# A hybrid decoder trunk on one core: the output projection's products move to another PSUM ring, the top-k search takes its bits out by shift and xor, and attention advances by more steps per feed-forward unit

## The chip, the cores and the metric

The kernel runs as one program on one NeuronCore of a Trainium2 chip. The metric is the time of one execution on the device, in microseconds (us). The core has five engines that run side by side, each through its own list of instructions in order: TensorE (PE in the profile; PEld are its weight loads) multiplies matrices into PSUM, VectorE (DVE), ScalarE (ACT) and GpSimd (POOL) do the elementwise work, and SyncE (SP) starts most DMA transfers. An engine waits where an input, or a buffer to write to, isn't ready.

## The reference

A sequence of 1024 tokens of width 1024 goes through two layers. Each has a token mixer and a squared-ReLU feed-forward part ("MLP" below), with RMS norms before and after. Layer 0 mixes with a state-space model (S5), layer 1 with sparse attention. Everything is float32.

```python
for i in range(2):
    pre = rms_norm(h, g[i, 0])
    mix = s5_mixer(pre, ...) if i == 0 else dsa_mixer(pre, w_in, w_out)
    h = h + rms_norm(mix, g[i, 1])
    ff = square(relu(rms_norm(h, g[i, 2]) @ w1[i])) @ w2[i]        # 1024 -> 4096 -> 1024
    h = h + rms_norm(ff, g[i, 3])

def dsa_mixer(h, w_in, w_out):                                      # 16 heads, 4 key heads, 8 index heads
    q, k, v, qi, ki, wi = split(h @ w_in); rope on q, k, qi, ki
    for each block of 128 queries:
        score = sum over index heads of relu(qi . ki) * wi          # causal
        idx = top 256 keys of each query by score
        o = softmax(q . k[idx] / 8) @ v[idx]
    return o @ w_out                                                # the output projection
```

## The kernel before

**Tiling.** The sequence is cut into two halves of 512 tokens. Activations lie with features on the 128 partitions, so a product of a 128x128 weight piece and 512 tokens is one matmul. A float32 product is made of three passes (`mm3`, lines 157 to 159): weights and activations are split into a high and a low part, and high x high, high x low and low x high add up in PSUM. `unit` loads 128x1024 weights and splits them: ScalarE makes the high part (line 140), VectorE or GpSimd the low part (line 141). One unit feeds 24 matmuls.

**Stages.** S5 for both halves; the MLP of layer 0 for half 0; the MLP of layer 0 for half 1, beside which the index projection, the projections and the attention of half 0 run; the MLP of layer 1 for half 0, beside which those of half 1 run; and the MLP of layer 1 for half 1 alone. Blocks 0 to 3 of 128 queries belong to half 0, blocks 4 to 7 to half 1.

**What runs beside an MLP.** `mlp` takes a generator (`side`). After each of its 64 units it advances the generator by `per` steps, and the instructions of these steps are given a priority ahead of the MLP's. `PER_B` lists the steps per unit for the stages beside layer 1's first MLP: projections with scores, search over blocks 4 and 5, scores of 6 and 7, search over 6 and 7 with attention of 4 and 5, attention of 6 and 7. `hold(n)` makes the generator wait for n units. What order the instructions of an engine finally have is set by a scheduler of the framework, which goes by priorities, by dependences, and by the pools: each tag of a pool has some buffers, given out in turn.

**PSUM.** The MLP's products take tiles of the tag `m` (`pm`, 3 buffers, "m" in the profile). Scores, attention, projections and the rope transposes of `att_r` take tiles of the tag `p1` (`p1`, "p" in the profile). Norms take tiles of the tag `c`.

**The norms between the MLPs.** When the MLP of layer 0 ends for half 1, `post_norm` sums squares (VectorE line 191, then small matmuls on line 194), takes the reciprocal root (lines 165 to 169), spreads it with transposes (line 236), copies it (ScalarE, line 238), scales (line 250) and adds the residual (line 260). `pre_norm` then scales by the gain (lines 206 and 207) and sums squares again (lines 184 to 194, line 212). `att_r` multiplies the rope tables by the norm's factor (line 1144) and transposes them (line 1153). Behind it in the program stand `att_out`, the output projection of half 0's attention, whose 8 tiles come from 24 matmuls each and leave PSUM by ScalarE (line 1124), and `index` for half 1. The same `att_out` runs a second time, for half 1, at the end of the generator.

**The search.** `topk` finds the 256th largest score of each query by bits. The score's bit pattern, as an integer, is built from bit 30 down. For each bit, `cand` is the current value with that bit set (line 966); VectorE counts the scores at or above it in one block (line 936), ScalarE in the other by summing signs of score minus candidate (line 974, for which line 970 makes the negative candidate); line 979 compares the two counts with what is wanted, and line 980 copies the candidate over the current value where the count suffices. There are three searches of two blocks each, 31 bits each.

## Time and profile before

| | |
|---|---|
| time, median of 3 runs | 2286.31 us (2282.1 to 2287.16) |
| the profiled execution: time, span | 2287.54 us, 2285.6 us |
| granted clock of TensorE, mean over the span | 0.971 |
| TensorE busy | 2166.6 us (95%), 10376 matmuls |
| VectorE busy | 1436.7 us (63%) |
| ScalarE busy | 1083.0 us (47%) |
| GpSimd busy | 701.8 us (31%) |

Lines of a timeline read: start in us, duration in us, engine, line, operation, written tile <- read tiles, size of an operand, count; in square brackets the idle time of the engine before it, and what ended that. Rows of a table by shape read: line, engine, operation, tiles, shapes, count, then busy us in all and mean ns of one, then idle us ahead of them and its main cause. A window's row reads: from:to, length, then for each engine the busy us and the number of instructions, and at the end the granted clock, the DMA engines' share and GB/s. A busy TensorE is also one that runs at half its clock, so a window is to be read with the clock beside it.

### The profile page before, as it was taken

Reading aid. Unit: us, or ns where it says so; the run is one execution under the profiler, and the core shown is the slowest. Engines: PE = TensorE matmul, PEld = TensorE weight load, DVE = VectorE, ACT = ScalarE, POOL = GpSimd, SP = SyncE. Lnnn points to the kernel's source line nnn. Section 1 sums busy time; section 2 is a strip of 40 time slices with the busy share of each in tenths; the row PEclk is TensorE's granted clock in tenths of the full one; section 3 lists DMA queues with packets and bytes.
Section 4 is the critical chain, followed back from the end, with each engine's and each line's share of the span. In section 5 each row is a group of like instructions: output and inputs, shape, how many; then the busy total and the mean of one; then the engine's idle time right before and its main releaser. Section 6 shows DMA issues by size and latency. Waiting matters only on the chain.

```text
span 2285.6 us, 29529 instructions
## 1 busy us (share of the span) xinstructions
PE 2166.6 (95%) x10376; PEld 1785.5 (78%) x10376; DVE 1436.7 (63%) x2775; ACT 1083.0 (47%) x2027; POOL 701.8 (31%) x588
## 2 busy tenths in 40 slices
PE   6999999999989999999988988999999899999996
PEld 3577778888878888888877766888788687888886
DVE  9566953333656598555677898989767467332335
ACT  4434643333353475555363455677457354423332
POOL 2004542222336522221346533221210035222223
PEclk9999999999999999999989999999999999999998
DMA  7002533333337653445346543433332444433231
GB/s 276 27 30 83 181 123 94 100 95 100 111 114 204 165 134 107 119 101 167 132 159 157 154 119 81 110 86 92 88 84 60 134 131 164 138 95 99 93 105 51
DMA packets 115893, 266.81 MB, mean 117 GB/s; under 512 B 14241, under 2 KB 49569, under 8 KB 115745
## 3 DMA queue, kind: packets, MB, share of 16 engines
q1 hardware_dynamic: 101984, 240.80, 33.9%
q0 software_dynamic: 12672, 23.07, 5.3%
q8 instruction: 82, 1.34, 0.3%
q10 hardware_dynamic: 1088, 1.05, 0.1%
q14 instruction: 67, 0.54, 0.1%
HBM read 229.02 MB, written 34.67 MB: 115 GB/s over the span
## 4 chain that ended last, share of the span: by engine, by line
PE 73%; DVE 15%; ACT 6%; issue 4%; DMA 1%; POOL 1%; SPq 0%; ACTq 0%; DVEq 0%; POOLq 0%
PE m L158 18%; PE m L157 18%; PE m L159 18%; PE p L1036 2%; PE p L1056 2%; PE p L157 2%; PE p L159 2%; PE p L158 2%; DVE wh L141 2%; PE p L1064 1%; DVE b L250 1%; PE p L1065 1%; ACT junk L974 1%; DVE b L207 1%; PE m L611 1%
## 5 line engine op out<-in xcount | busy, mean ns | idle before, releaser
L157 PE MATMUL m<-b,wh 128*128 128x512 f32 (+1 forms) x2208 | 860.5, 392 | 26.1 <-DVE acc L334 9.7
L158 PE MATMUL m<-b,wh 128*128 128x512 f32 (+1 forms) x2208 | 858.0, 391 | 4.6 <-DVE b L207 4.0
L159 PE MATMUL m<-b,wh 128*128 128x512 f32 (+1 forms) x2208 | 856.3, 390 | 4.3 <-DVE wh L141 4.3
L141 POOL TENSOR_TENSOR wh<-wr,wh 128x512 fp32r<-128x512 f32 (+1 forms) x346 | 448.7, 1302 | 1281.6 <-ACT wh L140 1261.6
L140 ACT ACTIVATE wh<-wr 128x512 fp32r<-128x512 f32 (+1 forms) x692 | 400.0, 592 | 503.2 <-PE m L159 413.9
L157 PEld LDWEIGHTS m<-b,wh 128*128 128x128 f32 x2208 | 419.4, 190 | 115.8 <-DVE acc L334 10.8
L159 PEld LDWEIGHTS m<-b,wh 128*128 128x128 f32 x2208 | 418.9, 190 | 88.8 <-DVE wh L141 5.1
L158 PEld LDWEIGHTS m<-b,wh 128*128 128x128 f32 x2208 | 419.2, 190 | 87.3 <-DVE b L207 4.8
L141 DVE TENSOR_TENSOR wh<-wr,wh 128x512 fp32r<-128x512 f32 (+1 forms) x346 | 273.4, 797 | 296.8 <-ACT wh L140 283.2
L334 DVE TENSOR_TENSOR acc<-acc,m 128x512 f32<-128x512 f32 x216 | 147.1, 682 | 155.5 <-PE m L159 153.5
L299 ACT ACTIVATE b<-m 128x512 f32<-128x512 f32 x128 | 76.2, 595 | 179.0 <-PE m L159 175.8
L148 DVE CAST b<-b 128x1024 fp32r<-128x1024 f32 x68 | 59.9, 881 | 135.5 <-ACT b L301 126.4
L159 PE MATMUL p<-b,wh 128*128 128x512 f32 (+1 forms) x304 | 116.1, 391 | 8.4 <-DVE wh L141 8.4
L157 PE MATMUL p<-b,wh 128*128 128x512 f32 (+1 forms) x304 | 115.8, 398 | 5.7 <-ACT b L721 3.4
L158 PE MATMUL p<-b,wh 128*128 128x512 f32 (+1 forms) x304 | 117.3, 391 | 0.0
L1043 ACT ACTIVATE s<-s,ring 128x128 f32<-128x128 f32 (+7 forms) x128 | 98.6, 772 | 36.6 <-DVE ring L1040 35.4
L1061 DVE TENSOR_TENSOR pt<-p,pt 128x512 fp32r<-128x512 f32 (+1 forms) x160 | 99.1, 630 | 22.3 <-ACT pt L1060 22.0
L1060 ACT ACTIVATE pt<-p 128x512 fp32r<-128x512 f32 (+1 forms) x160 | 83.5, 551 | 60.4 <-PE p L1056 59.5
L974 ACT ACTIVATE junk<-b,ring 128x512 bf16<-128x512 f32 (+2 forms) x90 | 80.7, 896 | 64.8 <-DVE ring L970 59.4
L1036 PE MATMUL p<-kt,q 128*128 128x512 f32 (+2 forms) x384 | 100.2, 365 | 1.5 <-DVE pt L1061 1.2
L1056 PE MATMUL p<-con,s 128*128 128x128 f32 x576 | 93.1, 273 | 0.0
L1040 DVE CUSTOM_DVE_ANT_0 s<-p,nb 128x512 f32<-128x512 f32 (+3 forms) x128 | 72.6, 582 | 25.4 <-PE p L1036 25.2
(304 smaller groups left out, 2738.0 us busy)
## 6 DMA issues: line engine op xcount, KB each, us to landing
wr<-in_w_dram SPq DMA_DIRECT2D x256, 512.0 KB, 3.6
wr<-in_wa_dram SPq DMA_DIRECT2D x32, 512.0 KB, 3.7
q<-qd POOLq DMA_DIRECT2D x64, 256.0 KB, 5.4
ld<-hd SPq DMA_DIRECT2D x24, 512.0 KB, 6.2
hd<-b SPq DMA_DIRECT2D x16, 512.0 KB, 4.4
qd<-b SPq DMA_DIRECT2D x128, 64.0 KB, 2.1
wr<-in_wao_dram SPq DMA_DIRECT2D x16, 512.0 KB, 3.6
q<-qi POOLq DMA_DIRECT2D x24, 256.0 KB, 4.8
```

The lines of the kernel that those rows point to most:

```text
L140: nc.scalar.activation(ph, pr, AF.Copy)
L141: (nc.gpsimd if h else nc.vector).tensor_sub(pl, pr, ph.bitcast(F32))
L157: mm(ps, w[0], x[0], start=start, stop=False)
L158: mm(ps, w[0], x[1], start=False, stop=False)
L159: return mm(ps, w[1], x[0], start=False, stop=stop)
L334: nc.vector.tensor_add(acc[d][:, j], acc[d][:, j], ps)
L974: nc.scalar.activation(junk[:, 1, :W[j]], keys[j].bitcast(F32), AF.Sign, bias=neg[:, j:j + 1], accum_out=cnt[:, j:j + 1])
L1036: nc.tensor.matmul(ps[:, :m], qt[:, v, 2 * hp + k, :], self.K[c][g // 2][:, g % 2, :m], start=v == 0, stop=v == 1)
L1043: nc.scalar.activation(s, s, AF.Exp, bias=least, scale=-1.0, accum_out=self.sums[:, h:h + 1])
L1056: nc.tensor.transpose(pt[:, kk, k, :], P[k][:, (k0 + kk) * 128:(k0 + kk + 1) * 128], self.ident)
L1060: nc.scalar.activation(ph[:, :nk], pt[:, :nk], AF.Copy)
L1061: nc.vector.tensor_sub(pl[:, :nk], pt[:, :nk], ph.bitcast(F32)[:, :nk])
```

## The change

It has three parts. In `topk`, the current value starts at 1<<30 and is itself the candidate. For each bit an xor prepares the value with the next lower bit set; the counts are now of scores below the candidate, and where too many are below, one instruction shifts the comparison's 1 to the bit's place and takes the bit out by xor. ScalarE gets its sign of candidate minus score by a scale of -1, so no negative candidate is made. `att_out` takes its PSUM tiles from `p1` and no longer from `m`, in both of its calls. And the steps per MLP unit become (8, 7, 8, 7, 6), with four units of hold ahead of half 1's `att_in`, 4 steps per unit from there, and one unit in each hold of `att_in`, as before.

```diff
-PER_B = (7, 6, 7, 6, 6)
+PER_B = (8, 7, 8, 7, 6)
-WAIT_OUT = 1
+WAIT_OUT = 4
...
-        def count(dst, j, thr):
-            ts(junk[:, 0, :W[j]], scs[j], thr, None, op0=ALU.is_ge, op1=ALU.add, accum_out=dst[:, j:j + 1])
+        def count(dst, j, thr, op=ALU.is_ge):
+            ts(junk[:, 0, :W[j]], scs[j], thr, None, op0=op, op1=ALU.add, accum_out=dst[:, j:j + 1])
...
-        kap2 = self.small([128, 4], F32, "kept")
+        lim, lim2 = [self.small([128, 4], F32, "kept") for _ in range(2)]
         for j in range(n):
+            ts(lim[:, j:j + 1], kap[:, j:j + 1], -1.0, float(W[j]), op0=ALU.mult, op1=ALU.add)
             if j in on_act:
-                ts(kap2[:, j:j + 1], kap[:, j:j + 1], 2.0, -float(W[j]), op0=ALU.mult, op1=ALU.add)
+                ts(lim2[:, j:j + 1], kap[:, j:j + 1], -2.0, float(W[j]), op0=ALU.mult, op1=ALU.add)
             else:
-                nc.vector.tensor_copy(kap2[:, j:j + 1], kap[:, j:j + 1])
-        cur = self.small([128, 4], I32, "kept")
-        nc.vector.memset(cur, 0)
+                nc.vector.tensor_copy(lim2[:, j:j + 1], lim[:, j:j + 1])
+        cur = S(I32)
+        nc.vector.memset(cur[:, :n], 1 << 30)
         for bit in range(30, -1, -1):
-            cand = S(I32)
-            ts(cand[:, :n], cur[:, :n], 1 << bit, None, op0=ALU.bitwise_or)
-            cf = cand.bitcast(F32)
-            if bit and on_act:
-                neg = S()
-                ts(neg[:, :n], cf[:, :n], -1.0, None, op0=ALU.mult)
-            cnt = S()
+
+            cf, cnt, m, nx = cur.bitcast(F32), S(), S(I32), cur
+            if bit:
+                nx = S(I32)
+                ts(nx[:, :n], cur[:, :n], 1 << (bit - 1), None, op0=ALU.bitwise_xor)
             for j in range(n):
                 if j in on_act and bit:
-                    nc.scalar.activation(junk[:, 1, :W[j]], keys[j].bitcast(F32), AF.Sign, bias=neg[:, j:j + 1],
-                                         accum_out=cnt[:, j:j + 1])
+                    nc.scalar.activation(junk[:, 1, :W[j]], keys[j].bitcast(F32), AF.Sign, bias=cf[:, j:j + 1],
+                                         scale=-1.0, accum_out=cnt[:, j:j + 1])
                 else:
-                    count(cnt, j, cf[:, j:j + 1])
-            m = S(I32)
-            tt(m[:, :n], cnt[:, :n], (kap2 if bit else kap)[:, :n], op=ALU.is_ge)
-            nc.vector.copy_predicated(cur[:, :n], m[:, :n], cand[:, :n])
+                    count(cnt, j, cf[:, j:j + 1], ALU.is_lt)
+            tt(m[:, :n], cnt[:, :n], (lim2 if bit else lim)[:, :n], op=ALU.is_gt)
+            cur = S(I32)
+            stt(cur[:, :n], m[:, :n], bit, nx[:, :n], op0=ALU.logical_shift_left, op1=ALU.bitwise_xor)
             yield
...
-                ps = self.pm()
+                ps = self.p1([128, 512])
...
             yield from self.attention_b(masks)
-            xo = yield from self.att_in(1, "b", WAIT_OUT)
+            yield from self.hold(WAIT_OUT)
+            self.per = 4
+            xo = yield from self.att_in(1, "b", 1)
             yield from self.att_out(xo, "b")
```

The scheduler sets the order anew for the changed program. Three places of it follow. Lines behind 963 have other numbers there; 1123, 1152 and 1063/1064 are 1124, 1153 and 1064/1065 of before.

TensorE at the end of the MLP of layer 0 for half 1. Before, on the way from that MLP to the index projection, the last rows of `att_out` (tile m_9441, its eighth) stand directly ahead of the rope transposes, and p_1453 behind them is the index projection's first tile:

```order
L157 MATMUL m_9441<-b_9043,wh_1_9438 128x512
L158 MATMUL m_9441<-b_9044,wh_1_9438 128x512
L159 MATMUL m_9441<-b_9043,wh_1_9438 128x512
L1153 MATMUL p_1428_9174<-con,b_9175 128x128 x4
L1153 MATMUL p_1430_9182<-con,b_9183 128x128 x4
L157 MATMUL p_1453_9475<-b_9119,wh_0_9469 128x512
```

Now the MLP's last tile (m_8982) is followed by the norms' matmuls and the rope transposes, and `att_out` (its first tile is p_1435) begins behind them:

```order
L159 MATMUL m_8982<-b_8704,wh_1_8965 128x512
L194 MATMUL c_9048<-con,b_9032 128x1 x4
L236 MATMUL c_9059<-con,ring 128x128 x4
L194 MATMUL c_9130<-con,b_9114 128x1 x4
L1152 MATMUL p_1429_9145<-con,b_9146 128x128 x4
L1152 MATMUL p_1431_9153<-con,b_9154 128x128 x4
L157 MATMUL p_1435_9171<-b_8996,wh_0_9165 128x512
L158 MATMUL p_1435_9171<-b_8997,wh_0_9165 128x512
```

All 192 matmuls of `att_out` moved from among the norms' small matmuls to behind the rope transposes.

VectorE inside the search over blocks 4 and 5, two bits of it, before (`ring` holds the small values, `con` the kept ones, sc_10140 is block 5's scores):

```order
L979 TENSOR_TENSOR ring<-ring,con 128x2
L980 COPY_PREDICATED con<-ring 128x2
L966 TENSOR_SCALAR ring<-con 128x2
L970 TENSOR_SCALAR ring<-ring 128x2
L936 TENSOR_SCALAR junk_10410,ring<-sc_10140,ring 128x768
L141 TENSOR_TENSOR wh_0_11274<-wr_11272,wh_0_11274 128x512
L979 TENSOR_TENSOR ring<-ring,con 128x2
L980 COPY_PREDICATED con<-ring 128x2
L966 TENSOR_SCALAR ring<-con 128x2
L970 TENSOR_SCALAR ring<-ring 128x2
```

And now:

```order
L977 TENSOR_TENSOR ring<-ring,con 128x2
L979 SCALAR_TENSOR_TENSOR ring<-ring 128x2
L970 TENSOR_SCALAR ring<-ring 128x2
L936 TENSOR_SCALAR junk_10381,ring<-sc_10111,ring 128x768
L141 TENSOR_TENSOR wh_0_11102<-wr_11100,wh_0_11102 128x512
L977 TENSOR_TENSOR ring<-ring,con 128x2
L979 SCALAR_TENSOR_TENSOR ring<-ring 128x2
L970 TENSOR_SCALAR ring<-ring 128x2
```

Four small rows of a bit are three: 977 is the comparison, 979 the shift and xor, 970 the xor ahead of the next count. From the search's first count to its last mask VectorE's list has 21 rows of line 141 before (15 of a whole half unit, and 6 narrow ones of the projections' units by heads, two to a unit) and 17 now (13 and 4); rows of line 334 go from 4 to 1, of which 3 lie in the profile's window of the search, and rows of line 148 from 2 to 3.

TensorE at the end of half 1's attention, where the tiles p_2797, p_2799 and p_2802 belong to the second `att_out`, now:

```order
L1063 MATMUL p_2753_14997<-pt_15039,v_11176 128x256
L1064 MATMUL p_2753_14997<-pt_15039,v_11176 128x256
L157 MATMUL p_2797_15314<-b_15198,wh_0_15308 128x512
L157 MATMUL p_2799_15348<-b_15198,wh_0_15342 128x512
L157 MATMUL p_2802_15383<-b_15198,wh_0_15377 128x512
L158 MATMUL p_2797_15314<-b_15199,wh_0_15308 128x512
```

Before, the tiles at this place are m_15440, m_15474 and m_15509, and the rows are otherwise the same: attention's last product and the output projection's first stand next to each other in both. Ahead of this place, attention's last stretch without an MLP matmul is 354 matmuls long before and 301 now, and 1 MLP unit of 24 matmuls stands among the second `att_out`'s products in both.

## The prediction

> **What bounds the kernel now.** I read the page first, then TensorE's timeline at each place where it stops, and then, for each place, the rows of the engine that it waits for. The page:
>
> ```profile
> span 2285.6 us, 29529 instructions
> PE 2166.6 (95%) x10376; PEld 1785.5 (78%) x10376; DVE 1436.7 (63%) x2775; ACT 1083.0 (47%) x2027; POOL 701.8 (31%) x588
> PE 73%; DVE 15%; ACT 6%; issue 4%; DMA 1%; POOL 1%; SPq 0%; ACTq 0%; DVEq 0%; POOLq 0%
> ```
>
> TensorE is busy for 95% of the span and holds 73% of the chain that ended last. The change does not alter its work, so only its stops can move the time. The stretches that matter, by windows (columns: length, then busy time of TensorE, its weight loads, VectorE, ScalarE, GpSimd, the granted clock, DMA):
>
> ```profile
> 800.00:892.00 92.00, 90.82 (x444) 76.39 (x443) 82.65 (x292) 62.72 (x161) 25.23 (x26) 1.00 0.48 120
> 1168.10:1175.00 6.90, 6.90 (x28) 5.60 (x27) 1.17 (x3) 1.91 (x4) 0.00 (x0) 0.81 0.28 78
> 1200.00:1225.00 25.00, 18.74 (x69) 14.39 (x68) 20.01 (x23) 5.86 (x14) 22.23 (x18) 0.80 0.50 124
> 1294.00:1411.00 117.00, 97.26 (x436) 78.20 (x435) 107.88 (x263) 59.97 (x128) 39.44 (x32) 0.94 0.37 104
> 1411.00:1725.00 314.00, 310.42 (x1656) 265.38 (x1655) 255.15 (x617) 196.64 (x377) 76.94 (x73) 1.00 0.36 92
> 1725.00:1784.80 59.80, 55.24 (x363) 47.64 (x362) 48.73 (x113) 45.20 (x85) 3.66 (x5) 0.97 0.21 54
> 1784.80:1792.70 7.90, 0.29 (x4) 0.09 (x2) 1.84 (x3) 1.44 (x2) 0.00 (x0) 0.74 0.78 196
> 1792.70:1798.80 6.10, 5.53 (x12) 3.94 (x13) 4.59 (x4) 2.11 (x2) 0.00 (x0) 0.50 0.91 246
> ```
>
> From 1294 to 1411, the search over blocks 4 and 5, VectorE is busy for 107.88 of 117 us and TensorE idle for 19.74: there VectorE sets the pace. From 1411 to 1725, with the third search, TensorE is idle for 3.6 of 314. At the end of attention it stops for 7.9 us, and after that stop it has half its clock for 6.1 us.
>
> The place that decides, though, is one where TensorE hardly stops: the first output projection, beside the norms between the two feed-forward parts. TensorE's rows there:
>
> ```profile
> 1113.62 0.39 PE L159 MATMUL m<-b,wh 128*128 128x512 f32 x1
> 1113.84 0.39 PE L157 MATMUL m<-b,wh 128*128 128x512 f32 x1
> ...
> 1120.42 0.95 PE L194 MATMUL c<-con,b 128*128 128x1 f32 x8
> ...
> 1127.26 0.60 PE L236 MATMUL c<-con,ring 128*128 128x128 f32 x4
> ...
> 1156.23 1.08 PE L194 MATMUL c<-con,b 128*128 128x1 f32 x8 [2.05 <-DVE b L191]
> ...
> 1163.36 0.39 PE L159 MATMUL m<-b,wh 128*128 128x512 f32 x1
> 1165.22 0.66 PE L1153 MATMUL p<-con,b 128*128 128x128 f32 x4 [1.46 <-ACT b L1151]
> 1167.32 1.12 PE L1153 MATMUL p<-con,b 128*128 128x128 f32 x4 [1.44 <-ACT b L1151]
> 1168.08 0.78 PE L157 MATMUL p<-b,wh 128*128 128x512 f32 x1
> ```
>
> The last feed-forward product starts at 1113.62. From 1113.84 to 1163.36 run the 192 products of the output projection (8 tiles of 24), and the norms' small matmuls (L194, L236) slip in between. The rope transposes (L1153) and the index projection follow. VectorE meanwhile walks the norm chain:
>
> ```profile
> 1115.43 1.22 DVE L191 TENSOR_TENSOR b<-b,b 128x512 f32<-128x512 f32 x1 [0.70 <-ACT b L187]
> ...
> 1121.40 0.16 DVE L232 TENSOR_TENSOR ring<-c,con 128x4 f32<-128x4 f32 x1 [3.23 <-PE c L194]
> ...
> 1122.54 0.16 DVE L169 SCALAR_TENSOR_TENSOR ring<-ring 128x4 f32<-128x4 f32 x1
> ...
> 1128.53 8.58 DVE L250 SCALAR_TENSOR_TENSOR acc<-acc,con,rb 128x512 f32<-128x512 f32 x8 [3.98 <-ACT rb L238]
> 1137.04 0.68 DVE L141 TENSOR_TENSOR wh<-wr,wh 128x512 fp32r<-128x512 f32 x1
> 1137.64 4.54 DVE L260 TENSOR_TENSOR acc<-acc,ld 128x1024 f32<-128x1024 f32 x2
> 1142.11 0.68 DVE L141 TENSOR_TENSOR wh<-wr,wh 128x512 fp32r<-128x512 f32 x1
> 1142.71 5.10 DVE L207 SCALAR_TENSOR_TENSOR b<-acc,con,b 128x512 fp32r<-128x512 f32 x6
> 1147.74 0.68 DVE L141 TENSOR_TENSOR wh<-wr,wh 128x512 fp32r<-128x512 f32 x1
> 1148.34 1.40 DVE L207 SCALAR_TENSOR_TENSOR b<-acc,con,b 128x512 fp32r<-128x512 f32 x2
> 1149.66 0.68 DVE L191 TENSOR_TENSOR b<-b 128x512 f32<-128x512 f32 x1
> 1150.44 5.64 DVE L191 TENSOR_TENSOR b<-b,b 128x512 f32<-128x512 f32 x6
> ...
> 1162.56 0.15 DVE L212 TENSOR_SCALAR con<-c 128x4 f32<-128x4 f32 x1
> ```
>
> The reader sees a chain of some 50 us that costs about 6 us of TensorE's time, because the output projection covers it. Matmuls run in their written order: L194's input was ready at 1115.43 + 1.22 = 1116.65, and it ran at 1120.42, behind the products written ahead of it.
>
> **The change, part by part.**
>
> *The output projection's PSUM, first call.* By the order of the built program the 192 products no longer stand among the norms' matmuls. TensorE has: last feed-forward product, L194, L236, L194, both rope transposes, and only then the first product. Its tiles now come from the ring out of which att_r, written ahead of att_out, takes its two. So the cover is gone, and the chain stands bare. Its length, step by step from the rows above:
> - from 1113.84 to the end of the squares' sum at 1116.65: 2.8.
> - L194 to L169's end: 1120.42 to 1122.70, 2.3.
> - L236 to the start of L250: 1127.26 to 1128.53, 1.3. The waits of both matmuls behind products (3.8 and 4.6 us) fall away.
> - L250 to the last square added: 1128.53 to 1156.08, 27.55, less three weight splits (L141, 0.6 each of their own) that move behind the chain: 25.7.
> - L194 to L212 as at 1120.42 to 1121.40: 1.0; L212 to the first rope transposes, 1162.56 to 1165.22, less one 0.57 of another norm's squares: 2.1.
> - first transposes to the product behind them, 1165.22 to 1168.08: 2.9.
>
> Together 38.1 us in which TensorE has 24 tiny matmuls. Then come the products, 192 x 0.227 (the distance of two starts, as at 1113.62 and 1113.84) = 43.6. They start after a long stop, so I charge what the other long stop shows, 6.1 us at clock 0.50, a loss of 3.05. The index projection then starts at 1113.84 + 38.1 + 43.6 + 3.05 = 1198.6 against 1168.08: 30.5 later. Two things come back: its products ran in a window of 6.9 us at clock 0.81, 0.19 of it lost, and no stop stands ahead of them now (-1.3); and behind it the order has 12 more query products ahead of the first feed-forward product that needs the next norm, 2.7 us of cover where TensorE was idle for 6.3 of 25 us (1200 to 1225). I take half, -1.4. **Chain: +27.7.** Low end: the adds and scalings run 3 us faster with no GpSimd splits beside them, +24.5; high end: neither gain comes, and half clock lasts longer, +32.
>
> By the Trainium skill (TensorE: Matmul & The Clock Gate, "The HAM clock gate") an idle window of about 3.4 us halves the clock and one busy window of 3.4 us restores it. The trace agrees that the clock halves, but took 6.1 us to restore it; by the page the loss would be an estimated 1.7 rather than 3.05, and the sum 1.35 less.
>
> *The search.* Per bit the candidate, its negation, the comparison and the predicated copy become an xor, the comparison and one shift-and-xor; the negation goes. The costs, VectorE by shape, from 1293 to 1410:
>
> ```profile
> L141 DVE TENSOR_TENSOR wh<-wr,wh 128x512 fp32r<-128x512 f32 x15 | 11.7, 783 | 0.0
> L970 DVE TENSOR_SCALAR ring<-ring 128x2 f32<-128x2 f32 x30 | 11.0, 367 | 0.9
> L980 DVE COPY_PREDICATED con<-ring 128x2 int32<-128x2 int32 x31 | 8.8, 284 | 0.9
> L141 DVE TENSOR_TENSOR wh<-wr,wh 128x256 fp32r<-128x256 f32 x6 | 4.0, 685 | 0.0
> L334 DVE TENSOR_TENSOR acc<-acc,m 128x512 f32<-128x512 f32 x3 | 2.0, 683 | 0.4 <-PE m L159 0.4
> ```
>
> 30 negations at 0.367 are 11.0 us of VectorE in each search. The shift-and-xor is not in the trace; it takes 128x2 as its neighbours do, so it lies between L980's 0.284 and L970's 0.367: over 31 bits 0 to +2.6, I take 0. The second search alone stands where VectorE sets the pace. The first (800 to 892) lies under TensorE's 90.82 of 92 us and the third under its 310.42 of 314; were that cover gone, each would give 11 us too.
>
> *More steps to a unit* takes feed-forward units out of just this stretch: between the search's first count and its last mask the order has 21 weight splits before and 17 now, and three accumulator adds fewer. That is 2 x 0.783 + 2 x 0.685 + 3 x 0.683 - 0.8 (one cast more, taken at a split's size) = 4.2 us of VectorE less, but three units (the narrow splits come two to a unit) of 24 x 0.227 = 5.45 us less for TensorE. Before, 15 + 3 units: 117 - 18 x 5.45 = 18.9 idle, close to the 19.74 seen. Now: 117 - 11.0 - 4.2 - 15 x 5.45 = 20.1. The shorter stretch holds as much idle time as the longer one, so by this count nothing is won; if the moved units fill other gaps, all 11 is. **Search and steps: -4**, nearer the count; bounds -11, and +4 where the units land where TensorE was full.
>
> *End of attention.* The four units of hold do not fill the stop: in the order the first product of the second output projection still follows the last of attention's.
>
> ```profile
> 1784.80 0.27 PE L1065 MATMUL p<-pt,v 128*128 128x256 f32 x1
> 1792.69 1.65 PE L157 MATMUL m<-b,wh 128*128 128x512 f32 x3 [7.61 <-ACT b L1108]
> ```
>
> The stop waits for attention's sums to go out and come back, which nothing here shortens: 0. Ahead of it the order has 301 matmuls of attention without a feed-forward one among them, where it had 354; 15% of that stretch's idle 4.56 and of its clock loss (0.03 x 60) is about -1; bounds -4 (feed-forward work spread well) and +2.
>
> Sum: 27.7 - 4 - 1 = +22.7 on the profiled execution's 2287.54, 2310.2. The median shown is 1.2 lower (2286.31), so I predict **2309 us**, 1.0% slower. 0.2%, some 4.6 us, is about what a measurement of this kernel can tell from no change.
>
> **Rivals.**
> - *The search pays in full* and the chain is at its short end: 24.5 - 11 - 4 = +9.5, **2296**. For it: VectorE's 92% busy; against: the count of units. 22%.
> - *The bare chain is dear*: 32 + 4 + 2 = +38, **2324**. For it: TensorE also lacked clock from 1200 to 1225 (0.80). 13%.
> - *VectorE pays everywhere*, faster than before: if VectorE and not TensorE limits the three searches, 3 x 11.0 = 33 comes off against 27.7: **2281**. It decides once 84% of VectorE's saving appears in the span. Against: TensorE's 3.6 us of idle time in the third search. 6%.
> - *The search's stop closes wholly*: 19.74 idle and 0.06 x 117 = 7.0 of clock cancel the chain to +1 us: **2287**, no difference. 4%.
>
> The forecast, 2303 to 2316, keeps 55%. Slower: 55 + 22 + 13 = 90%; same 4%; faster 6%. Range 2297 to 2320: it cuts the outer half of the first two rivals, and leaves out about 2 in 10.
>
> **What would show it.** Right: in TensorE's rows a stop of 35 to 40 us, broken by L194, L236 and L194 alone, between the last feed-forward product and the first product of the first output projection, waited for by L191 and the rope copy; the clock at 0.5 around it; from the index projection on everything some 28 us later. The search's idle time should stay at 15 to 20 us in a stretch some 15 us shorter, and the stop of 7 to 8 us after attention should remain. Wrong: if products of the output projection run between L194 and the transposes, the chain's term falls and the result is a gain of a few us; if the search's stretch loses its idle time, the first or last rival holds.

## The result, and the profile after

| | before | changed |
|---|---|---|
| time, median | 2286.45 us, 4 runs (2282.1 to 2287.16) | 2309.63 us, 4 runs (2304.71 to 2314.63) |
| the profiled execution: time, span | 2287.54 us, 2285.6 us | 2304.71 us, 2302.8 us |
| granted clock, mean over the span | 0.971 | 0.968 |
| TensorE busy | 2166.6 us | 2167.0 us |
| VectorE busy | 1436.7 us | 1420.1 us |

The ratio of the changed kernel to the one before is 1.0106, with a 95% interval of 1.008 to 1.0131: slower, by about 23 us. Forecast were 2309 us and a range of 2297 to 2320. The profiled execution of the changed kernel is the fastest of its four; that of before is a little slow among all its runs (the 73 of the three experiment batches have medians of 2283.92, 2284.41 and 2285.21). So the two traces differ by 17 us where the medians differ by 23, and a term of a few us that is read from the two traces alone is no more certain than that.

TensorE's work is the same (10376 matmuls in both); its stops are longer. Where, its timeline between the last MLP product of layer 0 and the first product of the output projection tells:

```profile
1116.41 0.39 PE L159 MATMUL m<-b,wh 128*128 128x512 f32 x1
1119.47 1.87 PE L194 MATMUL c<-con,b 128*128 128x1 f32 x8 [2.67 <-DVE b L191]
1122.72 1.09 PE L236 MATMUL c<-con,ring 128*128 128x128 f32 x4 [1.39 <-DVE ring L169]
1147.06 1.84 PE L194 MATMUL c<-con,b 128*128 128x1 f32 x8 [23.25 <-DVE b L191]
1151.38 1.12 PE L1152 MATMUL p<-con,b 128*128 128x128 f32 x4 [2.49 <-ACT b L1150]
...
1154.53 0.78 PE L157 MATMUL p<-b,wh 128*128 128x512 f32 x1
...
1199.15 0.39 PE L157 MATMUL p<-b,wh 128*128 128x512 f32 x1
...
1204.59 0.95 PE L194 MATMUL c<-con,b 128*128 128x1 f32 x8
```

Before, 192 products of the output projection stood between these rows. Now TensorE has nothing but the norms' matmuls and the transposes from 1116.64 (1116.41 and the 0.227 from one product's start to the next) to 1154.53, 37.9 us; the 192 products follow up to 1199.15, where the index projection starts. One wait of 23.25 us holds most of it, for VectorE's L191, whose rows in that stretch are:

```profile
1118.22 1.19 DVE L191 TENSOR_TENSOR b<-b,b 128x512 f32<-128x512 f32 x1 [0.70 <-ACT b L187]
...
1124.47 7.47 DVE L250 SCALAR_TENSOR_TENSOR acc<-acc,con,rb 128x512 f32<-128x512 f32 x8 [1.90 <-ACT rb L238]
...
1142.38 4.53 DVE L191 TENSOR_TENSOR b<-b,b 128x512 f32<-128x512 f32 x6
1148.93 0.16 DVE L212 TENSOR_SCALAR con<-c 128x4 f32<-128x4 f32 x1 [2.02 <-PE c L194]
```

It is the same chain as before, with none of TensorE's products beside it. The other places that the prediction spoke of, by windows (length, busy time of TensorE, its loads, VectorE, ScalarE, GpSimd, clock, DMA). First the start of the products behind the stop, then the stretch from the index projection's norm to the first scores, the 31 bits of the second search, the third search, the end of attention, and the stop behind it:

```profile
1154.50:1158.00 3.50, 3.50 (x13) 2.86 (x12) 0.00 (x0) 1.19 (x2) 0.00 (x0) 0.69 0.00 0
1205.00:1256.00 51.00, 45.12 (x195) 36.28 (x196) 47.29 (x52) 22.17 (x45) 42.77 (x34) 0.93 0.51 151
1323.00:1409.00 86.00, 72.67 (x332) 58.35 (x332) 78.76 (x190) 50.45 (x109) 31.48 (x26) 0.94 0.39 111
1421.00:1735.00 314.00, 307.68 (x1632) 260.32 (x1631) 257.45 (x593) 200.06 (x382) 77.02 (x71) 1.00 0.36 92
1735.00:1799.20 64.20, 60.97 (x396) 52.91 (x395) 50.41 (x115) 45.25 (x87) 4.90 (x6) 1.00 0.28 72
1799.20:1805.40 6.20, 0.55 (x4) 0.34 (x3) 2.04 (x3) 1.44 (x2) 0.00 (x0) 0.71 0.95 241
```

And of before, the two of these that the prediction cut otherwise (the same rows of the program, from the index projection's norm to the scores, and from the second search's first comparison to its last):

```profile
1175.00:1231.50 56.50, 47.41 (x197) 38.08 (x196) 47.44 (x52) 22.63 (x45) 42.50 (x34) 0.85 0.52 150
1301.80:1396.10 94.30, 79.89 (x371) 65.00 (x370) 88.61 (x222) 52.98 (x113) 33.63 (x27) 0.95 0.38 107
```

The stretch ahead of the scores gave something back: idle 5.88 us at clock 0.93 against 9.09 at 0.85. The search's bits became 8.3 us shorter, with 39 matmuls fewer, and TensorE is idle for 13.3 us of them against 14.4.

### The profile page after: what moved, and what is told of

Same layout as the page of the kernel before. It is cut to its first block, busy times and chain, and to the rows that moved or that the text cites. A ratio compares the mean times of both kernels' runs of the same rounds, so it can differ in the third digit from the quotient of the medians.

```text
span 2302.8 us, 29428 instructions
## 1 busy us (share of the span) xinstructions
PE 2167.0 (94%) x10376; PEld 1784.4 (77%) x10376; DVE 1420.1 (62%) x2688; ACT 1084.6 (47%) x2027; POOL 719.1 (31%) x588
## 4 chain that ended last, share of the span: by engine, by line
PE 75%; DVE 13%; ACT 5%; issue 4%; DMA 2%; POOL 2%; SPq 0%; DVEq 0%; ACTq 0%; POOLq 0%
PE m L157 17%; PE m L159 17%; PE m L158 17%; PE p L157 3%; PE p L158 3%; PE p L159 3%; PE p L1055 2%; PE p L1035 2%; PE p L1064 1%; PE p L1063 1%; DVE b L250 1%; PE m L611 1%; ACT junk L973 1%; DVE wh L141 1%; DVE b L207 1%
## 5 line engine op out<-in xcount | busy, mean ns | idle before, releaser
L141 POOL TENSOR_TENSOR wh<-wr,wh 128x512 fp32r<-128x512 f32 (+1 forms) x346 | 466.3, 1352 | 1309.7 <-ACT wh L140 1303.6
L157 PE MATMUL m<-b,wh 128*128 128x512 f32 (+1 forms) x2080 | 813.7, 391 | 8.9 <-ACT b L299 4.8
L159 PE MATMUL m<-b,wh 128*128 128x512 f32 (+1 forms) x2080 | 810.8, 390 | 8.3 <-DVE wh L141 8.3
L158 PE MATMUL m<-b,wh 128*128 128x512 f32 (+1 forms) x2080 | 809.8, 389 | 4.0 <-DVE b L207 4.0
L157 PEld LDWEIGHTS m<-b,wh 128*128 128x128 f32 x2080 | 394.0, 189 | 91.9 <-ACT b L299 7.7
L159 PEld LDWEIGHTS m<-b,wh 128*128 128x128 f32 x2080 | 394.0, 189 | 87.6 <-DVE wh L141 9.1
L141 DVE TENSOR_TENSOR wh<-wr,wh 128x512 fp32r<-128x512 f32 (+1 forms) x346 | 262.9, 766 | 315.4 <-ACT wh L140 305.5
L158 PEld LDWEIGHTS m<-b,wh 128*128 128x128 f32 x2080 | 394.1, 189 | 81.3 <-DVE b L207 4.8
L157 PE MATMUL p<-b,wh 128*128 128x512 f32 (+1 forms) x432 | 161.0, 395 | 9.7 <-ACT b L1107 5.7
L158 PE MATMUL p<-b,wh 128*128 128x512 f32 (+1 forms) x432 | 161.9, 389 | 0.5 <-DVE b L1108 0.5
L159 PE MATMUL p<-b,wh 128*128 128x512 f32 (+1 forms) x432 | 159.4, 388 | 2.8 <-DVE wh L141 2.8
L1060 DVE TENSOR_TENSOR pt<-p,pt 128x512 fp32r<-128x512 f32 (+1 forms) x160 | 99.2, 631 | 28.2 <-ACT pt L1059 27.7
L1059 ACT ACTIVATE pt<-p 128x512 fp32r<-128x512 f32 (+1 forms) x160 | 83.4, 552 | 67.6 <-PE p L1055 62.9
L157 PEld LDWEIGHTS p<-b,wh 128*128 128x128 f32 x432 | 83.7, 195 | 27.4 <-ACT b L1107 5.9
L159 PEld LDWEIGHTS p<-b,wh 128*128 128x128 f32 x432 | 82.7, 192 | 20.1 <-DVE wh L141 3.7
```

Of the source, the lines that this page charges most:

```text
L141: (nc.gpsimd if h else nc.vector).tensor_sub(pl, pr, ph.bitcast(F32))
L157: mm(ps, w[0], x[0], start=start, stop=False)
L158: mm(ps, w[0], x[1], start=False, stop=False)
L159: return mm(ps, w[1], x[0], start=False, stop=stop)
L1059: nc.scalar.activation(ph[:, :nk], pt[:, :nk], AF.Copy)
L1060: nc.vector.tensor_sub(pl[:, :nk], pt[:, :nk], ph.bitcast(F32)[:, :nk])
```

## The experiments

All ratios are to the kernel before, run beside each experiment. In brackets stand the lowest and the highest time and, behind a ratio, its 95% interval. Two groups take the change apart, and a third asks what the search's idle time is made of.

### The ring: which of its uses, and why

**The ring alone.** The kernel before, with only the output projection's PSUM changed, in both calls:

```diff
-                ps = self.pm()
+                ps = self.p1([128, 512])
```

> The kernel before with nothing changed but the ring of the output projection's products. Lost cover: +27, about 2313, with a stop of about 38 us between the last feed-forward product of layer 0 and the projection's first. Rival, search or steps are what costs: 2286.

Measured: 2305.11 us (2303.88 to 2308.14), ratio 1.01 (1.0085 to 1.0115). That is +21.2 us, where 27 was expected, and the ring by itself carries nearly all of the change's price. TensorE's timeline of it:

```profile
1110.08 0.39 PE L159 MATMUL m<-b,wh 128*128 128x512 f32 x1
...
1139.92 1.84 PE L194 MATMUL c<-con,b 128*128 128x1 f32 x8 [23.25 <-DVE b L191]
...
1147.39 0.78 PE L157 MATMUL p<-b,wh 128*128 128x512 f32 x1
...
1198.67 0.95 PE L194 MATMUL c<-con,b 128*128 128x1 f32 x8
```

It is the same stop (37.1 us) with the same single wait of 23.25 us. The last row is the index projection's norm, behind the 192 products and 24 more.

**All but the ring.** The changed kernel with the output projection back on `m`:

```diff
-                ps = self.p1([128, 512])
+                ps = self.pm()
```

> The changed kernel with the output projection's products back in the ring of m (both calls); search and steps stay changed. Lost cover (my theory): the bare norm chain goes, 2309.6 - 27 = about 2283, 2278 to 2287. Rival, search or steps are what costs: stays above 2300. TensorE shows no stop over 5 us between 1100 and 1170 us.

Measured: 2287.38 us (2282.42 to 2289.94), ratio 1.0015 (1.0006 to 1.0023): +3.5 us, where a gain was expected. The search and the steps together cost a little, which is the second group's question. The two halves add up to the whole: 21.2 + 3.5 = 24.7, and the change measured 23.2.

**The order of requests, with the ring as in the change.** The first output projection is written ahead of `att_r`, so that it asks for its tiles of `p1` before the rope transposes do:

```diff
-        self.att_r(1, r)
         for _ in self.att_out(xo, "hid"):
             pass
+        self.att_r(1, r)
         fA = self.F
```

> The changed kernel with the first output projection written ahead of the rope transposes of att_r, its products still in the ring of p1. Lost cover through the ring's turn: it asks the ring first, the products stand among the norms again and 27 us come back, about 2283. Rival, that the ring p1 itself (shared with attention, more buffers in turn) is what delays the products: the stop stays and the time is about 2309.

Measured: 2287.78 us (2282.78 to 2291.28), ratio 1.0019 (1.001 to 1.0028), the same as with `m`. Its timeline (here without the rows of the products, lines 157 to 159) has no stop left but the old one of 2 us; L194 and L236 wait for nothing that a bracket shows, since products stand ahead of them:

```profile
1123.93 0.95 PE L194 MATMUL c<-con,b 128*128 128x1 f32 x8
...
1130.78 0.60 PE L236 MATMUL c<-con,ring 128*128 128x128 f32 x4
...
1159.75 1.02 PE L194 MATMUL c<-con,b 128*128 128x1 f32 x8 [2.05 <-DVE b L191]
```

So `p1` as such costs nothing. What costs is to stand in the same ring behind a request that can only be served at the end of the norm chain.

**The first call on `m`, the second on `p1`.**

```diff
-    def att_out(self, x, ftag):
+    def att_out(self, x, ftag, ring=None):
...
-                ps = self.p1([128, 512])
+                ps = ring() if ring else self.p1([128, 512])
...
-        for _ in self.att_out(xo, "hid"):
+        for _ in self.att_out(xo, "hid", self.pm):
```

> The changed kernel, but the first of the two output projections takes its PSUM from m again; the second stays on p1. If the ring's whole price lies at the first call, this is the kernel with both calls on m: 2287 us (2285 to 2289). Rival: the second call on p1 has a price or a gain of its own. In the changed kernel's trace the stop behind attention was 5.8 us against 7.6 with both on m, which would give 2285; a price like that of the first call's would show as over 2291.

Measured: 2288.19 us (2279.29 to 2291.11), ratio 1.0016 (1.0004 to 1.0028), as with both on `m`. The second call's ring does nothing: the stop behind attention is here

```profile
1791.01 1.65 PE L157 MATMUL p<-b,wh 128*128 128x512 f32 x3 [7.41 <-ACT b L1107]
```

7.41 us, and 7.51 with both calls on `m`. By these traces the 5.7 us of the changed kernel's are not due to the ring.

**The transposes moved to the other ring.** The changed kernel, with the two tiles of `att_r` taken from `m`, and both output projections on `p1` in their place:

```diff
-            ps = self.p1([128, 4, 128])
+            ps = self.pm().rearrange("p (t n) -> p t n", t=4)
```

> The changed kernel with one thing exchanged: the two tiles of the rope transposes come from m, while both output projections keep p1 and their place in the program. If the 38 us stop comes from sharing a ring with the transposes that are asked for ahead of it, the products stand among the norms' matmuls again and the time is that of the two other versions with cover: 2287 us (2284 to 2290). Rival: it is the place in the program that counts, the stop stays and the time is the changed kernel's, 2305 to 2312. Second rival: cover comes back, but the transposes on m now delay the index projection, and half of the gain is lost: 2295 to 2300.

Measured: 2304.52 us (2301.25 to 2305.53), ratio 1.0083 (1.007 to 1.0096). By the time alone the first rival, 2305 to 2312, would nearly stand. The trace tells another story. `att_r` is called twice, and the edit moved both calls. At the output projection the stop is gone; no wait of TensorE there is longer than this one:

```profile
1182.29 1.11 PE L194 MATMUL c<-con,b 128*128 128x1 f32 x8 [2.04 <-DVE b L191]
```

At the first call, between the MLP of layer 0 for half 0 and that for half 1, there is a new one:

```profile
596.82 0.39 PE L159 MATMUL m<-b,wh 128*128 128x512 f32 x1
...
627.41 1.83 PE L194 MATMUL c<-con,b 128*128 128x1 f32 x8 [23.19 <-DVE b L191]
631.73 1.11 PE L1152 MATMUL m<-con,b 128*128 128x128 f32 x4 [2.49 <-ACT b L1150]
...
634.88 0.78 PE L157 MATMUL m<-b,wh 128*128 128x512 f32 x1
```

It is the very same stop, 37.8 us, in another place: there the products behind the transposes are the next MLP's, which come from `m`. None of the three expectations foresaw this, since none of them looked at the first call; the mechanism, a ring shared with the transposes, is shown twice by it, once by a stop that goes and once by one that comes.

### The search and the steps

**The new search alone**, the kernel before with the changed `topk` and nothing else. Of its diff the core:

```diff
-            tt(m[:, :n], cnt[:, :n], (kap2 if bit else kap)[:, :n], op=ALU.is_ge)
-            nc.vector.copy_predicated(cur[:, :n], m[:, :n], cand[:, :n])
+            tt(m[:, :n], cnt[:, :n], (lim2 if bit else lim)[:, :n], op=ALU.is_gt)
+            cur = S(I32)
+            stt(cur[:, :n], m[:, :n], bit, nx[:, :n], op0=ALU.logical_shift_left, op1=ALU.bitwise_xor)
```

> The kernel before with the search by shift and xor alone; steps and rings as before. If VectorE's 11 us of the second search come out in full because no feed-forward unit is moved out of that stretch: 2286 - 11 = 2275, and the idle time of TensorE in the search falls from 20 to about 9 us. If the scheduler moves units anyway or another wait takes over: 2282 to 2287. If VectorE paid in all three searches: 2253.

Measured: 2283.1 us (2279.75 to 2288.53), ratio 0.9995 (0.9984 to 1.0006), no difference. First, the instructions were shortened less than the prediction charged. VectorE's small rows of all three searches, before:

```profile
L970 DVE TENSOR_SCALAR ring<-ring 128x2 f32<-128x2 f32 x90 | 25.0, 277 | 2.0
L980 DVE COPY_PREDICATED con<-ring 128x2 int32<-128x2 int32 x93 | 21.1, 227 | 2.1
L966 DVE TENSOR_SCALAR ring<-con 128x2 int32<-128x2 int32 x93 | 19.8, 215 | 2.3
L979 DVE TENSOR_TENSOR ring<-ring,con 128x2 int32<-128x2 f32 x93 | 18.0, 194 | 12.7 <-ACT junk L974 10.0
```

and with the new search:

```profile
L977 DVE TENSOR_TENSOR ring<-ring,con 128x2 int32<-128x2 f32 x93 | 23.8, 256 | 9.7 <-ACT junk L973 7.4
L979 DVE SCALAR_TENSOR_TENSOR ring<-ring 128x2 int32<-128x2 int32 x93 | 20.7, 223 | 2.0
L970 DVE TENSOR_SCALAR ring<-ring 128x2 int32<-128x2 int32 x90 | 18.4, 204 | 2.2
```

83.9 us became 62.9: 21 us less in three searches, not 33. The negation's 0.367 us is its mean in the second search; over all three it is 0.277, and 25.0 us in all. Of these some 10 us are time in which it was held beside an instruction of GpSimd (the last section shows such rows), and what is held passes to other rows when one is taken out: the comparison rose from 18.0 us to 23.8. Second, what was saved did not reach the end. The second search:

```profile
1305.30:1388.60 83.30, 68.49 (x324) 56.25 (x323) 75.83 (x188) 48.72 (x106) 31.06 (x25) 0.94 0.40 114
```

11 us shorter than before, TensorE idle for 14.8 us instead of 14.4, and 47 matmuls fewer inside it. They run elsewhere, and the time shows no gain from that.

**The new steps alone**, in the kernel before:

```diff
-PER_B = (7, 6, 7, 6, 6)
+PER_B = (8, 7, 8, 7, 6)
...
-            xo = yield from self.att_in(1, "b", WAIT_OUT)
+            yield from self.hold(WAIT_OUT)
+            self.per = 4
+            xo = yield from self.att_in(1, "b", 1)
```

with `WAIT_OUT` 4 as in the change.

> The kernel before with only the new steps per unit, the four units of hold and the 4 steps behind them; search and output projection as before. The output projection on its own ring with the new search and the new steps measured +3.5 us, the new search alone -0.8, so if costs add the steps cost +4.3: 2288 us (2286 to 2291). The prediction's own count said more: three units of 5.45 us leave the second search for places where TensorE is full, less 4.2 us of VectorE: +12, 2296 us. Rival: the steps do nothing alone, and the 3.5 us come from the two together: 2284 us.

Measured: 2287.79 us (2283.46 to 2293.31), ratio 1.0012 (1.0001 to 1.0023): +3.4 us, with an interval that reaches from almost nothing to 5. With the search's -0.8 this gives 2.6, near the 3.5 of both together. The steps are the small loss, as far as runs with this spread can tell; the count of three units that would cost 12 us was far too dear.

**Fewer steps to a unit in the second search**, with the new search: if too little work stands beside its bits, this should bring more of it there.

```diff
-PER_B = (7, 6, 7, 6, 6)
+PER_B = (7, 4, 7, 6, 6)
```

> The kernel before with the new search, and 4 instead of 6 steps per feed-forward unit in the second search alone. Theory: the search shortened VectorE's work, but the order holds work for TensorE only in proportion to the bits, so the idle time stayed at 21 us; with half again as many units beside the same bits the idle time falls. Some 2 to 3 more units of 5.45 us (11 to 16 us of TensorE's work) in a stretch that grows by the 3 x 1.6 us of their splits on VectorE at most: 2271 to 2278 us, idle time of the second search 8 to 14 us. Rival: each bit waits for its own chain and VectorE is full; the added units stretch the search by as much as they fill: 2281 to 2286 us, idle time still about 20 us.

Measured: 2297.73 us (2288.75 to 2301.38), ratio 1.0062 (1.0044 to 1.008), slower, which neither theory expected. The search hardly changed (335 matmuls in 85.6 us, against 324 in 83.3). The loss came behind it: from the first product of attention over block 4 to the last of attention the two kernels' windows, of the new search alone and then of this one, read

```profile
1432.90:1780.30 347.40, 343.18 (x1928) 294.77 (x1927) 278.03 (x679) 228.82 (x433) 70.08 (x67) 1.00 0.32 85
```

```profile
1421.00:1805.00 384.00, 371.08 (x2029) 317.35 (x2027) 288.41 (x689) 237.21 (x448) 75.46 (x71) 0.99 0.30 83
```

idle 12.9 us against 4.2. This profiled execution is the fastest of its six, 9 us under their median, so much of the loss is in none of the traces and stays unexplained.

**One search step instead of two between two steps of the projections**, with the new search:

```diff
-STEPS_BEST = 2
+STEPS_BEST = 1
```

> The kernel before with the new search, and one search step instead of two between two steps of the projections of half 1, so that the search spreads over more of the projections' products. If the idle time of the second search comes from too little work beside it, it falls as with more feed-forward units: 2270 to 2278 us. Rival: the projections' units bring VectorE work of their own (narrow splits), or are used up before the search begins and nothing changes: 2281 to 2288 us.

Measured: 2282.59 us (2278.62 to 2287.03), ratio 0.9994 (0.9984 to 1.0004), no difference. Its second search is 26 us shorter than that of before, and TensorE is idle for 13.6 us of it against 14.4:

```profile
1315.20:1383.30 68.10, 54.47 (x249) 42.24 (x248) 62.56 (x174) 46.56 (x98) 17.24 (x13) 0.95 0.32 93
```

### What the search's idle time is

In each version the 31 bits of the second search read, by windows from the first comparison to the last (idle is the length less TensorE's busy time; the 20 and 21 us that some expectations name are larger counts, not over the bits alone). The last three rows are the versions described below.

| version | length, us | matmuls inside | TensorE idle, us | clock | time against before |
|---|---|---|---|---|---|
| before | 94.3 | 371 | 14.4 | 0.95 | |
| steps alone | 96.7 | 363 | 16.7 | 0.95 | +3.4 |
| changed kernel | 86.0 | 332 | 13.3 | 0.94 | +23.2 |
| all but the ring | 85.1 | 326 | 13.5 | 0.94 | +3.5 |
| new search alone | 83.3 | 324 | 14.8 | 0.94 | -0.8 |
| ... and 4 steps to a unit | 85.6 | 335 | 13.5 | 0.92 | +13.3 |
| ... and one search step at a time | 68.1 | 249 | 13.6 | 0.95 | -1.8 |
| new search, narrow splits on GpSimd | 80.9 | 320 | 10.9 | 0.92 | -8.2 |
| new search, all splits on GpSimd | 84.9 | 311 | 17.3 | 0.90 | +11.4 |
| ... and one search step at a time | 68.0 | 228 | 14.9 | 0.92 | +2.4 |

The idle time belongs neither to the length nor to the number of bits' instructions: from 68 to 97 us it stays between 13 and 17 in the first seven versions. Only moving splits between engines takes it out of that range. In the trace it is a handful of single waits, most of them of 0.7 to 4.1 us, some at the same products in one version and the next. With the new search alone some of them are at the projections by heads, whose products read weights that are split in narrow pieces (TensorE by shape, from 1235 to 1420 us):

```profile
L158 PE MATMUL p<-wh,b 128*128 128x256 f32 x32 | 10.3, 324 | 3.1 <-DVE wh L141 3.1
L157 PE MATMUL p<-wh,b 128*128 128x256 f32 x32 | 10.0, 329 | 4.0 <-ACT wh L140 4.0
```

Three versions of the new search move splits away from VectorE.

**All narrow splits on GpSimd**, in the whole program; before, each unit had half of them there:

```diff
-                (nc.gpsimd if h else nc.vector).tensor_sub(pl, pr, ph.bitcast(F32))
+                (nc.gpsimd if h or heads else nc.vector).tensor_sub(pl, pr, ph.bitcast(F32))
```

> The kernel before with the new search, and the weight splits by heads (two narrow ones per half unit) all on GpSimd, where VectorE had half of them. In the second search TensorE's losses stand at a few single waits of 1.3 to 4.2 us, several of them for a split that stands in VectorE's list behind the counts. Theory: those of the narrow splits (3.1 us behind VectorE in the search's window) and the 4 us of VectorE time go: 2277 to 2280 us. Rival: the split waits for ScalarE's high part or for its turn anyway, or GpSimd slows VectorE: 2282 to 2286 us.

Measured: 2277.06 us (2274.73 to 2279.43), ratio 0.9966 (0.9954 to 0.9978). This is faster than both kernels, by 8.2 us against the one before. The same stretch of 185 us, with the new search alone and then with this:

```profile
1235.00:1420.00 185.00, 163.64 (x748) 134.16 (x747) 156.08 (x292) 99.27 (x214) 78.66 (x70) 0.96 0.46 128
```

```profile
1235.00:1420.00 185.00, 169.85 (x771) 138.87 (x770) 161.44 (x288) 103.66 (x223) 93.28 (x91) 0.96 0.49 136
L158 PE MATMUL p<-wh,b 128*128 128x256 f32 x32 | 10.3, 325 | 1.4 <-DVE wh L141 0.9 <-POOL wh L141 0.5
L157 PE MATMUL p<-wh,b 128*128 128x256 f32 x32 | 9.8, 322 | 2.3 <-ACT wh L140 2.3
```

6.2 us less idle time, 3.4 of it at the narrow products, and 23 more matmuls done in the same time. The theory's time, 2277 to 2280 us, came true.

**All splits on GpSimd while the second search runs**, narrow and wide, by a flag that is set ahead of the search and taken back behind it:

```diff
-                (nc.gpsimd if h else nc.vector).tensor_sub(pl, pr, ph.bitcast(F32))
+                (nc.gpsimd if h or self.searching else nc.vector).tensor_sub(pl, pr, ph.bitcast(F32))
...
+        self.searching = True
         yield from self.topk([4, 5], sc, masks, (4,))
+        self.searching = False
```

> The kernel before with the new search, and in the second search all weight splits on GpSimd (1.3 us each there, 0.8 on VectorE; some 12 wide and 4 narrow ones change over, 14 us of VectorE's time). Theory: VectorE sets the pace of this search, so it gets shorter by much of the 14 us and its idle time of 21 us for TensorE falls: 2270 to 2277 us. Rival, from the other versions: the idle time stays at 20 us whatever the search's length, less of TensorE's work falls into it, and the time stays: 2281 to 2286 us. Second rival: the splits become late on GpSimd, which takes longer for each and has the rope's sums to do: over 2288 us.

Measured: 2296.57 us (2288.72 to 2301.13), ratio 1.0047 (1.003 to 1.0064), slower; idle time in the search's 84.9 us 17.3, clock 0.90. The second rival gave the time; its reason, splits that are late on GpSimd, is only partly seen: 2.5 us more idle time than with the new search alone, and 1.2 us behind GpSimd's splits among the waits of the projections' products. More of these waits stand behind ScalarE's high parts, 11.3 us from 1300 to 1400 against 5.8 with the search alone. Nor did VectorE get free: 11 splits, 10 us of its time, left it, and it was busy for 77.8 us against 75.8, in part since many of its instructions are held when they start beside one of GpSimd's (the last section). By a count over the single rows they took some 21 us more in this search than such instructions usually do, against some 14. Where most of the 12 us between the two versions arise stays open.

**The same with one search step at a time.** The flag stays, and:

```diff
-STEPS_BEST = 2
+STEPS_BEST = 1
```

> The same with one search step instead of two between two steps of the projections. Alone this step order gave a search of 68 us with 20 us lost, and 2282.6 us. Theory: without splits on VectorE the search takes 55 to 60 us and loses 12 us or less: 2270 to 2276 us. Rival: the loss stays at 20 us: 2281 to 2285 us.

Measured: 2287.6 us (2281.83 to 2290.88), ratio 1.001 (0.9999 to 1.002), about 4 us worse than without the flag (+2.4 against -1.8); 14.9 us idle in 68.0. The rival's idle time stayed in kind (14.9 us against 13.6 of the same step order without the flag), its time was missed.

## Why the prediction came out, point by point

The total was right within a us, but two parts of it were wrong in opposite directions, and that they cancelled is luck. By the experiments' medians the chain was charged 6.5 us too much (27.7, measured 21.2 with an interval of 19 to 26), and the search, the steps and the end of attention 8.5 us too little (-4 and -1, measured +3.5 together).

- **That the cover goes, and why**: right. The stop was to be 38.1 us and is 37.9, broken by L194, L236 and L194 alone. That the shared ring does it, by the order in which tiles are asked for, is shown by the ring alone, by the projection written first, and by the transposes on `m`.
- **The stop's length step by step**: right in the sum by two errors. VectorE's part from L250 to the last square took 1142.38 + 4.53 - 1124.47 = 22.4 us and not 25.7, because no weight split of GpSimd held its instructions any more (the last section has rows). The prediction's low end had named this, with 3 us. The steps with small matmuls took 3 us longer than charged: L194 ran for 1.87 and 1.84 us, where 0.95 and 1.08 stood before, at a granted clock of 0.50 from 1119.4 us on.
- **The clock behind the stop**: mis-sized, 3.05 charged. The 192 products took 1199.15 - 1154.53 = 44.6 us against 43.6 at full clock, so 1.0 was lost. What I had taken for the size was one other stop's. In the ring-alone trace the same stop cost 2.3: from the first product to L194 stand 216 products, which took 1198.67 - 1147.39 = 51.3 us there against 49.0 at full clock, and 1204.59 - 1154.53 = 50.1 here. By the Trainium skill (TensorE: Matmul & The Clock Gate, "The HAM clock gate") the budget is about 3.4 us of time in windows that run free, so that the loss differs from one run to another; the estimate of 1.7 from it was nearer than mine, and the values here, 1.0, 2.3 and 3.05, lie on both sides of it.
- **What comes back behind it**: mis-sized. The index projection started 1199.15 - 1116.41 = 82.7 us behind the last MLP product, before 1168.08 - 1113.62 = 54.5: 28.3 later, where 30.5 was forecast, the difference being the clock. Its products at full clock then gave 1.4, where 1.3 was foreseen: L194 at 1204.59 stands 88.2 behind, before 61.3, which leaves 26.9. The cover of the next norm was charged at 1.4; from there to the scores the changed kernel took 5.5 to 6 us less, the 51.0 and 56.5 of the two windows above with nearly the same matmuls, by less idle time and more clock. That leaves some 21, by the trace of this one execution; the ring alone, by medians, says 21.2. In the ring-alone trace the same stretch gave back some 3 us, so how the 5.5 divide between the cover and chance is open.
- **The search**: the step that failed is the one that gave a sign to it. That the idle time stays (13.3 us, before 14.4) in a shorter stretch was right. The reason given, that the new steps take units out of this stretch, was not: with the search alone and the old steps 47 matmuls left it just the same, and with the steps alone only 8. When the bits get shorter, less work falls between them, and part of the idle time hangs on late splits. The size was off as well: 11.0 us for each search took the negation's mean of 0.367 for its price, but six of its 30 rows were held beside GpSimd, and the others took 0.17, which makes 5.1 us for 30. The first and third searches gave nothing that shows, as said: TensorE was busy for 307.68 of 314 us in the stretch with the third.
- **The steps**: -4 was for both parts together, and the steps by themselves cost +3.4. That lies near the bound of +4, "where the units land where TensorE was full", which I had as an end and not as the value. In the version with the steps alone TensorE's idle time in the second search rose by 2.3 us, which is the only part of it that a trace shows.
- **The end of attention**: ahead of the stop, where -1 was charged, TensorE was idle for 3.2 us at full clock (1735 to 1799.2) against 4.6 at 0.97 (0.03 x 60 = 1.8 lost) before, so this trace gave some 3 us, inside the bounds. The stop stayed, as forecast; the trace's 5.7 us against 7.6 before is not the ring's doing, as the version with only the second call on `p1` shows, and what it is stays open.
- **The rivals**: that the search pays in full, and that VectorE pays everywhere, fall with the search alone (-0.8, where they needed some -11 and -33). That the stop of the search closes falls by the table above. The dear chain falls by the clock and the cover.

## What to carry to other kernels

Before a product is given another PSUM ring, look at what is asked for ahead of it in that ring: a tile whose producer stands at the end of a long chain holds up every later request, and with it work that was ready and covered the chain; asking in the other order costs nothing. Time saved on an engine that shares a stretch with the bottleneck is worth only what the bottleneck waited for there, so read the single waits and what they wait for, not the busy share. Nor is an instruction's mean duration what its removal gives: look at its single rows, which can hold waits for another engine. Here 21 us off VectorE's small instructions gave nothing, and moving a few weight splits out from behind them gave some 7 us more than the search alone, which makes the fastest version 8 us faster than the kernel before. Two terms with errors of opposite sign can make a right total, so each should be measured by itself.

## What the runs showed of the hardware

**The norms' VectorE instructions are held when they start beside one of GpSimd's.** The squares of the norm chain, by shape, before (beside GpSimd's weight splits) and in the changed kernel (without them):

```profile
L191 DVE TENSOR_TENSOR b<-b,b 128x512 f32<-128x512 f32 x7 | 6.8, 977 | 0.6
```

```profile
L191 DVE TENSOR_TENSOR b<-b,b 128x512 f32<-128x512 f32 x6 | 4.2, 692 | 0.5
```

The means, 977 ns and 692, hide what happened. Five of the seven took 0.69 us before, as all six do in the changed kernel. The other two started while GpSimd ran a split; here is the first of them, with that split and the next square:

```profile
1152.65 1.30 POOL L141 TENSOR_TENSOR wh<-wr,wh 128x512 fp32r<-128x512 f32 x1 [6.05 <-ACT wh L140]
```

```profile
1152.69 1.80 DVE L191 TENSOR_TENSOR b<-b,b 128x512 f32<-128x512 f32 x1
1154.60 0.69 DVE L191 TENSOR_TENSOR b<-b,b 128x512 f32<-128x512 f32 x1
```

It ends 0.54 us behind the end of the split. In the same way one of the eight scalings of L250 and one of the eight of L207 took 1.78 us beside a split, where others took 0.74. These three instructions make 3.2 of the 3.3 us by which VectorE's part of the chain became shorter. GpSimd had five splits and two adds beside the chain before, and has the two adds now, which hold one L250 and one L260 in both kernels. By the Trainium skill (GPSIMD Engine Reference, "1. Specifications") the two engines share their interfaces to SBUF, with contention where a VectorE instruction has two inputs there; these rows have, and agree with it.

**The mean of a small instruction holds such waits too.** The negation of 128x2 took 367 ns on the mean in the second search and 277 over all three. Its rows in that search are of two sorts; here is one of each, and the GpSimd instruction beside which the second started:

```profile
1353.71 0.17 DVE L970 TENSOR_SCALAR ring<-ring 128x2 f32<-128x2 f32 x1
1355.53 1.29 DVE L970 TENSOR_SCALAR ring<-ring 128x2 f32<-128x2 f32 x1
```

```profile
1355.49 1.30 POOL L806 TENSOR_TENSOR b<-b,b 128x512 fp32r<-128x512 f32 x1 [2.04 <-ACT b L805]
```

Of the 30, 24 took 0.17 us. Six started while GpSimd ran, took 0.66 to 1.29 us, and ended within 0.03 us of the end of GpSimd's instruction. Not every instruction is held: six of the 31 counts in the same search (L936, 128x768) started beside GpSimd too and took 1.00 us like the others. The shift-and-xor, which I had put between 284 and 367, took 193 ns on the mean in the second search of the version with the search alone, and 279 in that of the changed kernel:

```profile
L979 DVE SCALAR_TENSOR_TENSOR ring<-ring 128x2 int32<-128x2 int32 x31 | 6.0, 193 | 0.9
```

```profile
L979 DVE SCALAR_TENSOR_TENSOR ring<-ring 128x2 int32<-128x2 int32 x31 | 8.6, 279 | 1.0 <-DVE ring L977 0.2
```

In the first, 30 of its 31 rows took 0.16 us and one 1.21; in the second 27 took 0.16 and four, again beside GpSimd, 0.68 to 1.25.
